# Output projection accumulated in PSUM, convolution evicted by ScalarE, mixes in six pieces, weight splits with priority

## Chip, cores and metric

One Trainium2 core runs the whole block. The metric is the time of one execution on the device in microseconds; every run was taken on the chip. The engines are TensorE (PE, and PEld for its weight loads), VectorE (DVE), ScalarE (ACT), GpSimd (POOL) and the DMA queue of SyncE (SP). Each engine takes its instructions in the order of its own queue and waits on semaphores at the head of it.

## The reference

A layer over 1024 tokens of width 1024 (float32), cut to what is computed:

```python
h = rmsnorm(x, g_pre_mix)
u, xc, bc, cc, q, k, v, f_logit, gate_logits = split(h @ w_in)
y_a = s5_mixer(u, ...)                       # complex diagonal scan, GELU, GLU
y_b = bc * conv3_causal(cc * xc, conv_w)     # short gated convolution, width 512
y_c = forgetting_attention(q, k, v, f_logit) # 8 heads of 64, causal
gates = sigmoid(gate_logits + b_gate)        # three times 1024 columns
merged = gates[0] * (y_a @ wa) + gates[1] * (y_b @ wb) + gates[2] * (y_c @ wc)
mix = merged @ w_out
x = x + rmsnorm(mix, g_post_mix)
h = rmsnorm(x, g_pre_mlp)
return x + rmsnorm(square(relu(h @ w_ff1)) @ w_ff2, g_post_mlp)
```

## The kernel before

Products are made from split operands: ScalarE writes the upper part of a weight or activation (a copy to fp32r), VectorE subtracts it from the source to get the lower part (`split`, line 72; `wsplit` for weights, line 204), and TensorE adds three products, upper with upper, upper with lower and lower with upper. A product is 128x128 by 128x512. A weight tile can be used in full only when its lower part is there.

The order is written out by a small planner. Phases are Python generators; `spawn(gen, delay)` enters one into an event queue, `poll` (line 102) runs what is due by a clock that counts modelled TensorE time alone, and a number that a generator yields is the delay of its next piece. `settle` runs all that is left. What is written in this order is then ordered again for each engine by the framework's scheduler, which goes by its own model of readiness and by priority (by default, earlier written is higher). Under `manual_schedule` the named engines keep the written order among the instructions of that block.

The stages, in order of time:

- To about 60 us: the 8 tiles of x (128 tokens each) are squared and summed, the reciprocal root comes from `rsqrt1` (line 79: eight small operations), `x_norm` (338) makes a diagonal matrix for each tile, and `x_tr` (361) multiplies by it, which scales and transposes at once. `x_split` writes hT, the transposed input, as upper and lower halves.
- To about 375 us: the input projections for u, then conv x, c, b and the gates through `proj_stream`, in two PSUM banks (tag `pj`), while the four quarters of S5 run beside them. `conv_cons` (799) empties the banks of the convolution: x by ScalarE; c by a VectorE multiplication with x; b by a VectorE multiplication with the convolved `ac`. GpSimd makes tables and some of the S5 operands.
- 375 to 430 us: the value projection (`v_group`, 869), under a manual order for VectorE and ScalarE, with 16 steps of gate projections ahead of the second weight split. A step is three products.
- To about 815 us: attention by 64 units, with the q, k and gate projections as filler for TensorE, and w_ff2's sums on GpSimd.
- To about 1005 us: the merge. `merge_item` (1217) takes two blocks of 128 columns of one branch: 24 products, then VectorE multiplies by the gate (loaded as `gl`), GpSimd adds to `ma`, and after the third branch the sum is split into mT. Between the merges of the first and the second half of the tokens stands the output projection of the first half, four `rows_item`s (1257) with four token tiles each: the first half of the contraction is copied by ScalarE to `acc`, the second is added to it by VectorE. There are 8 PSUM banks (`mps`, 1157).
- `mix` (1282) is spawned for each token tile after its projection: ScalarE's sum of squares and a root on GpSimd, scaling by g_post_mix, adding x, a second root, scaling to `hr`, and transposes. For the second half (`th` = 1) it also makes the operands T1 to T4 and B22 of the MLP.
- From 1005 us: the second half's output projection (two `rows_item`s and `wo_last`, 1357), then the MLP in a Strassen-like scheme over pairs of column blocks (`Pair`, 1429): first P1 and P2 of eight pairs (`prep_a`, `run_a`), which need only the first half, then the other products. From 1386 us the second matrix and the final norm.

`Item.split` (1191) splits a stage's weights; `run_items` (1196) splits item i+1 before item i runs and loads two ahead. Upper and lower weight tiles have three buffers each, raw weights two (tag `raw`).

Of the kernel before, what the change touches and what calls it, by code (L numbers as in the profile page):

```python
# [20 lines left out]
P = 128  # L21
# [17 lines left out]
def hybrid_layer(ctx, tc, a, out, dbg=None):  # L39
# [298 lines left out]
    def x_norm(t0, n):  # L338

        sl = slice(t0, t0 + n)  # L340
        rsqrt1(xrs[:, sl], xsq[:, sl], xtm[:, sl])
        for t in range(t0, t0 + n):
            dgs[t] = xp.tile([P, P], F, name=f"dg{t}", tag="dg", bufs=8)
            if t == 3:
                act.activation(dgs[t], ident, AF.Copy, scale=xrs[:, t:t + 1])
            else:
                ts(dgs[t], ident, xrs[:, t:t + 1], MUL)
# [24 lines left out]
    with tc.manual_schedule(engines={mybir.EngineType.DVE, mybir.EngineType.Activation}):  # L372
        for t in range(4):
            x_square(t)
            if t == 3:
# [14 lines left out]
        x_norm(4, 4)  # L390
# [408 lines left out]
    def conv_cons(which, j):  # L799
        def f(th, ps):  # L800
            sl = slice(th * HALF, (th + 1) * HALF)
            if which == "x":
                if th == 0:
                    cvt["xs"] = cv.tile([P, L], F, name=f"xs{j}", tag="xs")
                act.activation(cvt["xs"][:, sl], ps, AF.Copy)
            elif which == "c":
                if th == 0:
                    cvt["vp"] = cv.tile([P, L + 2], F, name=f"vp{j}", tag="vp")
                    pool.memset(cvt["vp"][:, 0:2], 0.0)
                vp = cvt["vp"]  # L810
                tt(vp[:, 2 + th * HALF:2 + (th + 1) * HALF], ps, cvt["xs"][:, sl], MUL)
                if th == 1:
                    ac = cvt["ac"] = cv.tile([P, L], F, name=f"ac{j}", tag="ac")
# [367 lines left out]
    class Item:  # L1181
# [33 lines left out]
    macc = {}  # L1215

    def merge_item(th, dp, b):
        def run(w):
# [15 lines left out]
            for d in range(2):  # L1234
# [16 lines left out]
                if b == 2:  # L1251
                    split(mT[0, th, dt_ // 4][:, dt_ % 4, :], mT[1, th, dt_ // 4][:, dt_ % 4, :], macc[d], scale=0.5)
# [4 lines left out]
    def rows_item(name, src_k, k0, e, toks, lhs, accumulate, after=None):  # L1257

        def run(w):
            for t in toks:  # L1260
                ps = mps(f"{name}p{t}")
                for k in range(4):
                    wh, wl = w[k // 2]
                    xh, xl = lhs(t, k)
                    mm(ps, xh, wh[:, k % 2, :], k == 0, False, 0.214)
                    mm(ps, xh, wl[:, k % 2, :], False, False, 0.214)
                    mm(ps, xl, wh[:, k % 2, :], False, k == 3, 0.214)
                dst = accs[t][:, e * HALF:(e + 1) * HALF]
                if accumulate:
                    tt(dst, ps, dst, ADD)  # L1270
                else:
                    act.activation(dst, ps, AF.Copy)
# [9 lines left out]
    def mix(t):  # L1282
# [10 lines left out]
        sp.dma_start(xr_, a["x"][t * P:(t + 1) * P, :])  # L1293
        hr = hrow[0](f"hr{t}")
        rs = rms_scale(acc, hr, f"n1_{t}")
        stt(acc, acc, rs, mixg[0], MUL, MUL)
        tt(acc, acc, xr_, ADD, dve if th else pool)
        yield MY1 if th else 8.0
        rs2 = rms_scale(acc, hr, f"n2_{t}")
        act.dma_start(x1_s[t], acc)  # L1300
        stt(hr, acc, rs2, mixg[1], MUL, MUL)
        c0 = (t % 4) * P
        cs = slice(c0, c0 + P)
        yield MY2 if th else 12.0
# [15 lines left out]
        else:  # L1320
# [22 lines left out]
    MY1, MY2 = 9.0, 12.0  # L1343
# [483 lines left out]
```

## Time and profile before

| | us |
|---|---|
| median of 3 runs | 1694.05 (1692.35 to 1694.09) |
| profiled execution | 1695.55 |
| its span, first to last instruction | 1693.8 |

The profile is of one execution. Its views are: the page with each engine's busy time; the waits, which put an engine's idle time down to what released it; windows, which give busy time and TensorE's granted clock (1.00 is 2.4 GHz, 0.50 is 1.2 GHz) of a stretch; the timeline of one engine, with the idle time ahead of an instruction and its releaser in brackets; groups by line; and the chain of work that ended last. Matmuls overlap, so the time of one is read from a long run of them.

### The profile page before, as it was taken

The numbers are of one execution on the slowest core, as the hardware profiler recorded it, in microseconds if no ns is written. First come the engines' busy times: TensorE is split into PE (matmuls) and PEld (weight loads), VectorE is DVE, ScalarE is ACT, GpSimd is POOL, SyncE is SP. The second block draws the span as 40 slices with busy tenths as digits, with TensorE's granted clock in tenths as the row PEclk, the third lists the DMA queues.
The fourth block names the chain that finished last, engine by engine and source line by source line (L and its number), as shares of the span: only waits on it lengthen the run. The fifth ranks groups of instructions, "written<-read, shape, count | busy, mean of one in ns | idle before, by whom it ended". The sixth has DMA issues, their size and how long they took to land.

```text
span 1693.8 us, 21052 instructions
## 1 busy us (share of the span) xinstructions
PE 1622.6 (96%) x7815; PEld 1334.8 (79%) x7815; DVE 1032.2 (61%) x1548; ACT 693.6 (41%) x1042; POOL 501.9 (30%) x603
## 2 busy tenths in 40 slices
PE   7999999999999999999999988799999999999997
PEld 6778778879878787877787777678778878888886
DVE  4768655333265463667583664778988764545665
ACT  5312122231354454556352333554354554444442
POOL 1085644100331403120153543244443300101143
PEclk9999999999999999999999989899999999999999
DMA  5412323330654616441782562456554599755521
GB/s 162 122 42 77 83 68 103 108 99 7 216 174 142 213 47 218 117 168 58 255 262 97 193 205 91 138 163 189 183 181 143 166 344 373 254 199 195 178 100 50
DMA packets 186034, 261.73 MB, mean 155 GB/s; under 512 B 24752, under 2 KB 108764, under 8 KB 183884
## 3 DMA queue, kind: packets, MB, share of 16 engines
q1 hardware_dynamic: 170380, 228.93, 41.8%
q10 hardware_dynamic: 15552, 31.46, 4.9%
q8 instruction: 61, 1.00, 0.2%
q14 instruction: 41, 0.34, 0.1%
HBM read 183.54 MB, written 75.63 MB: 153 GB/s over the span
## 4 chain that ended last, share of the span: by engine, by line
PE 64%; DVE 9%; POOL 5%; DMA 5%; issue 4%; ACT 3%; SPq 1%; DVEq 0%; ACTq 0%; POOLq 0%
PE p_g L122 13%; PE P L122 11%; PE pb L122 3%; PE p_q L122 3%; PE pv L122 3%; PE P4f L122 3%; PE P7f L122 3%; PE P3f L122 3%; PE P6f L122 3%; PE P5f L122 3%; PE P2f L122 3%; PE P1f L122 2%; PE ps L122 2%; PE av L122 2%; PE pt L126 2%
## 5 line engine op out<-in xcount | busy, mean ns | idle before, releaser
L65 DVE TENSOR_TENSOR st<-x,st 128x1024 fp32r<-128x1024 f32 x70 | 86.7, 1250 | 77.4 <-ACT st L73 74.4
L122 PE MATMUL p_g<-hT,w_g_1H 128*128 128x512 f32 x384 | 126.4, 407 | 5.1 <-ACT g L831 3.5
L122 PE MATMUL p_g<-hT,w_g_0H 128*128 128x512 f32 x384 | 126.9, 406 | 2.8 <-DVE ac L65 2.8
L73 ACT ACTIVATE st<-x 128x1024 fp32r<-128x1024 f32 x70 | 73.6, 1059 | 98.5 <-PE P6f L122 16.6
L65 POOL TENSOR_TENSOR w2s<-w2s 128x512 f32<-128x512 f32 x32 | 44.0, 1375 | 232.1 <-DMA w2s<-in_w_ff 232.1
L65 POOL TENSOR_TENSOR s<-w1r 128x512 f32<-128x512 f32 x32 | 52.4, 1659 | 167.4 <-DMA w1r<-in_w_ff 156.4
L122 PE MATMUL pb<-yH,wb_0L 128*128 128x512 f32 x192 | 77.5, 403 | 11.8 <-DVE wb_0L L65 11.7
L65 DVE TENSOR_TENSOR sl<-x,sh 128x1024 fp32r<-128x1024 f32 x42 | 56.6, 1352 | 47.4 <-ACT sh L73 47.4
L122 PEld LDWEIGHTS p_g<-hT,w_g_1H 128*128 128x128 f32 x384 | 69.3, 192 | 17.5 <-ACT g L831 4.0
L122 PEld LDWEIGHTS p_g<-hT,w_g_0H 128*128 128x128 f32 x384 | 70.0, 191 | 14.8 <-DVE ac L65 3.2
L122 PE MATMUL pb<-yH,wb_0H 128*128 128x512 f32 x192 | 77.0, 401 | 2.1 <-DVE macc L68 2.1
L65 POOL TENSOR_TENSOR fa<-fa,gfin 128x512 f32<-128x512 f32 x16 | 25.5, 1606 | 178.0 <-ACT fjk L1654 178.0
L122 PE MATMUL p_g<-hT,w_g_1L 128*128 128x512 f32 x192 | 76.6, 399 | 0.0
L122 PE MATMUL pb<-yL,wb_0H 128*128 128x512 f32 x192 | 76.6, 399 | 0.0
L122 PE MATMUL p_g<-hT,w_g_0L 128*128 128x512 f32 x192 | 76.5, 398 | 0.0
L65 DVE TENSOR_TENSOR PT<-pt,PT 128x512 fp32r<-128x512 f32 (+2 forms) x96 | 53.0, 552 | 26.7 <-ACT PT L73 26.1
L73 ACT ACTIVATE PT<-pt 128x512 fp32r<-128x512 f32 (+2 forms) x96 | 47.0, 490 | 47.9 <-PE pt L126 43.5
L73 ACT ACTIVATE sh<-x 128x1024 fp32r<-128x1024 f32 x42 | 44.2, 1058 | 51.4 <-PE P3f L122 9.9
L1023 ACT ACTIVATE P<-ps,mx 128x128 f32<-128x128 f32 (+3 forms) x64 | 47.4, 740 | 32.0 <-DVE mx L1020 31.9
L65 POOL TENSOR_TENSOR macc<-macc,gl 128x512 f32<-128x512 f32 x16 | 27.8, 1748 | 101.6 <-DVE gl L68 101.6
L1020 DVE TENSOR_REDUCE mx<-ps 128x1 f32<-128x128 f32 (+3 forms) x64 | 48.1, 752 | 13.2 <-PE ps L122 13.1
L122 PEld LDWEIGHTS pb<-yH,wb_0L 128*128 128x128 f32 x192 | 37.0, 193 | 21.7 <-DVE wb_0L L65 13.9
(831 smaller groups left out, 4631.6 us busy)
## 6 DMA issues: line engine op xcount, KB each, us to landing
w2s<-in_w_ff SPq DMA_DIRECT2D x16, 1024.0 KB, 5.0
w1r<-in_w_ff SPq DMA_DIRECT2D x16, 1024.0 KB, 8.6
as<-sa SPq DMA_DIRECT2D x16, 1024.0 KB, 6.8
x<-as SPq DMA_DIRECT2D x32, 512.0 KB, 10.8
x<-t_P SPq DMA_DIRECT2D x32, 512.0 KB, 5.3
r_g<-in_w_in SPq DMA_DIRECT2D x12, 1024.0 KB, 5.9
gt_s<-g ACTq DMA_DIRECT2D x48, 256.0 KB, 2.0
t_P<-w2s SPq DMA_DIRECT2D x48, 256.0 KB, 2.6
```

Source lines behind the costliest of these rows:

```text
L65: (eng or dve).tensor_tensor(o, x, y, op=op)
L73: act.activation(hi, src, AF.Copy, scale=scale)
L122: pe.matmul(o, l, r, start=start, stop=stop)
L126: pe.transpose(o, i, idn)
L1020: dve.tensor_reduce(mx, sv, axis=mybir.AxisListType.XY, op=MAX, negate=True)
L1023: act.activation(Pm[:, 0:kend].rearrange("p (c n) -> p c n", c=nch), sv, AF.Exp, bias=mx, accum_out=sm)
```

## The change

- Input: the roots are made one at a time for the first four tiles, that of tile 1 by GpSimd; the first weight split has its subtraction on VectorE instead of GpSimd. Tiles 4 to 7 are scaled in place (two by VectorE, two by ScalarE) and transposed with the identity.
- Convolution: ScalarE copies c and b out of PSUM; VectorE multiplies whole rows of 1024 in SBUF. The buffers are three, two and two in place of one each.
- Value projection: 12 gate steps ahead of the first weight split and 20 ahead of the second, where 0 and 16 were.
- `Item.split` and `prep_a` split under `high_priority`.
- The split of a merged block is an event of its own, 2 us after the sum was written.
- The output projection keeps its sum in PSUM over both halves of the contraction and is copied to `acc` once, by ScalarE.
- `mix` yields five times instead of two; T4 takes one VectorE operation less; the rows `hr` of tiles 6 and 7 no longer lie in a raw weight buffer but share two buffers with the others.
- P1 and P2 of the first eight pairs run two pairs at a time (`ff1_early`) with the same products, and `settle` follows them.

```diff
+    def x_rs(t0, n, eng=None):
         sl = slice(t0, t0 + n)
-        rsqrt1(xrs[:, sl], xsq[:, sl], xtm[:, sl])
+        rsqrt1(xrs[:, sl], xsq[:, sl], xtm[:, sl], eng)
...
-        mm(o, xt[t][:, kt * P:(kt + 1) * P], dgs[t], True, True, 0.22)
+        if t < 4:
+            mm(o, xt[t][:, kt * P:(kt + 1) * P], dgs[t], True, True, 0.22)
+        else:
+            transp(o, xt[t][:, kt * P:(kt + 1) * P], ident)
...
             x_square(t)
-            if t == 3:
-                ut_tiles[0].split(pool)
-            x_norm(t, 1)
+            x_rs(t, 1, pool if t == 1 else None)
             if t == 0:
+                x_diag(0)
                 dve.tensor_copy(gcol, pgc[:, 0:KT])
+            elif t == 2:
+                x_diag(1)
+                x_diag(2)
+        ut_tiles[0].split()
+        x_diag(3)
...
-        x_norm(4, 4)
+        x_rs(4, 4)
+        for t in range(4, NT):
+            if t % 2:
+                ts(xt[t], xt[t], xrs[:, t:t + 1], MUL)
+            else:
+                act.activation(xt[t], xt[t], AF.Copy, scale=xrs[:, t:t + 1])
...
-                tt(vp[:, 2 + th * HALF:2 + (th + 1) * HALF], ps, cvt["xs"][:, sl], MUL)
+                act.activation(vp[:, 2 + th * HALF:2 + (th + 1) * HALF], ps, AF.Copy)
                 if th == 1:
+                    tt(vp[:, 2:], vp[:, 2:], cvt["xs"], MUL)
...
-                ac = cvt["ac"]
-                tt(ac[:, sl], ps, ac[:, sl], MUL)
+                if th == 0:
+                    cvt["bs"] = cv.tile([P, L], F, name=f"bs{j}", tag="xs", bufs=3)
+                act.activation(cvt["bs"][:, sl], ps, AF.Copy)
                 if th == 1:
+                    ac = cvt["ac"]
+                    tt(ac, ac, cvt["bs"], MUL)
...
+        for _ in range(12):
+            next(ps_)
         split(wv[1][1], wv[1][2], wv[1][0])
-        for _ in range(16):
+        for _ in range(20):
             next(ps_)
...
-                self.w = [wsplit(self.raw[ix], shp, f"{self.name}_{i}") for i, (ix, shp) in enumerate(self.cuts)]
+                with tc.high_priority():
+                    self.w = [wsplit(self.raw[ix], shp, f"{self.name}_{i}") for i, (ix, shp) in enumerate(self.cuts)]
...
-                    split(mT[0, th, dt_ // 4][:, dt_ % 4, :], mT[1, th, dt_ // 4][:, dt_ % 4, :], macc[d], scale=0.5)
+                    spawn(merged(mT[0, th, dt_ // 4][:, dt_ % 4, :], mT[1, th, dt_ // 4][:, dt_ % 4, :], macc[d]), 2.0)
...
-                ps = mps(f"{name}p{t}")
+                if k0 == 0:
+                    wps[t, e] = mps(f"{name}p{t}")
+                ps = wps[t, e]
...
-                dst = accs[t][:, e * HALF:(e + 1) * HALF]
-                if accumulate:
-                    tt(dst, ps, dst, ADD)
-                else:
-                    act.activation(dst, ps, AF.Copy)
+                if k0:
+                    act.activation(accs[t][:, e * HALF:(e + 1) * HALF], ps, AF.Copy)
...
         sp.dma_start(xr_, a["x"][t * P:(t + 1) * P, :])
+        yield 1.5
         hr = hrow[0](f"hr{t}")
         rs = rms_scale(acc, hr, f"n1_{t}")
+        yield 5.0
         stt(acc, acc, rs, mixg[0], MUL, MUL)
         tt(acc, acc, xr_, ADD, dve if th else pool)
-        yield MY1 if th else 8.0
+        yield 2.5 if th else 5.0
         rs2 = rms_scale(acc, hr, f"n2_{t}")
         act.dma_start(x1_s[t], acc)
+        yield 5.0
         stt(hr, acc, rs2, mixg[1], MUL, MUL)
         c0 = (t % 4) * P
         cs = slice(c0, c0 + P)
-        yield MY2 if th else 12.0
+        yield 5.0
...
-            tt(tm[:, 1], b12, tk["D"][:, :, cs], ADD)
             tt(tm[:, 0], b22, tb[:, 1], SUB)
             tt(tb[:, 0], b22, tb[:, 0], SUB)
-            stt(tm[:, 1], b22, -1.0, tm[:, 1], MUL, ADD)
+            tt(tm[:, 1], tk["D"][:, :, cs], tb[:, 0], SUB)
...
-                    dst = accs[t][:, e * HALF:(e + 1) * HALF]
-                    tt(dst, ps, dst, ADD)
+                    act.activation(accs[t][:, e * HALF:(e + 1) * HALF], ps, AF.Copy)
...
-    hrow[0] = hr_tile
-    stages = ff1_stages()
+    hrow[0] = lambda name: r2.tile([P, D], F, name=name, tag="hr", bufs=2)
+    pairs = [Pair(i) for i in range(NF)]
+    stages = ff1_stages(pairs)
...
+    for i in range(0, KC, 2):
+        nxt = [p.prep_a for p in pairs[i + 2:i + 4]] if i + 2 < KC else [s_[0] for s_ in stages[:AH]]
+        for _ in ff1_early(pairs[i:i + 2], nxt):
+            poll()
+    settle()
```

## Rows read from the trace of the kernel before

**Rows 1.** The page: the span, then section 1, busy time of each engine.

```profile
span 1693.8 us, 21052 instructions
PE 1622.6 (96%) x7815; PEld 1334.8 (79%) x7815; DVE 1032.2 (61%) x1548; ACT 693.6 (41%) x1042; POOL 501.9 (30%) x603
```

**Rows 2.** Whom TensorE waited for: us in total, times, longest us.

```profile
PE P L122 <- DVE wa1L L65: 11.9, 1, 11.9
PE pb L122 <- DVE wb_0L L65: 11.7, 4, 7.2
PE p_cb L122 <- DVE vp L65: 3.7, 2, 2.6
PE p_g L122 <- ACT g L831: 3.5, 1, 3.5
PE p_g L122 <- DVE ac L65: 2.8, 1, 2.8
PE p_cx L122 <- DVE ac L65: 2.7, 1, 2.7
```

**Rows 3.** Windows: length; busy PE, PEld, DVE, ACT, POOL; granted clock; DMA.

```profile
111.50:115.00 3.50, 3.50 (x11) 2.68 (x10) 3.50 (x3) 0.00 (x0) 3.34 (x4) 0.52 0.05 11
206.60:210.00 3.40, 3.38 (x9) 2.73 (x10) 3.40 (x10) 0.20 (x1) 0.00 (x0) 0.60 0.39 160
251.00:254.50 3.50, 3.50 (x11) 2.69 (x11) 0.94 (x1) 0.00 (x0) 3.03 (x10) 0.59 0.80 251
373.00:377.00 4.00, 3.83 (x12) 3.03 (x13) 3.15 (x2) 1.86 (x3) 0.00 (x0) 0.69 0.57 160
926.50:930.50 4.00, 3.80 (x10) 2.98 (x11) 1.76 (x3) 0.00 (x0) 2.09 (x7) 0.62 0.41 131
979.50:985.30 5.80, 5.68 (x13) 4.47 (x14) 3.18 (x5) 1.12 (x3) 2.29 (x8) 0.50 0.91 314
1066.20:1071.50 5.30, 5.25 (x17) 4.18 (x18) 3.02 (x3) 2.25 (x5) 4.41 (x10) 0.56 0.77 201
84.00:88.00 4.00, 4.00 (x11) 3.14 (x10) 3.79 (x15) 0.00 (x0) 0.00 (x0) 0.53 0.06 18
```

**Rows 4.** Timeline of TensorE: start us, us; diagonal products, then transposes.

```profile
39.37 5.56 PE L122 MATMUL ptx<-dg,x 128*128 128x128 f32 x48
...
1070.68 1.11 PE L126 MATMUL pth<-ident,hr 128*128 128x128 f32 x8
```

**Rows 5.** Timeline of ScalarE before the second half is transposed; idle before in brackets.

```profile
38.20 0.69 ACT L369 ACTIVATE hT<-ptx,gcol 128x512 fp32r<-128x512 f32 x1 [4.87 <-PE ptx L122]
```

**Rows 6.** Timeline of VectorE in the convolution.

```profile
108.09 1.59 DVE L65 TENSOR_TENSOR CA<-CA,Cx 128x1152 f32<-128x1152 f32 x1 [6.26 <-POOL Cx L65]
```

**Rows 7.** Groups of ScalarE, 60 to 370 us: busy us, mean ns, idle before.

```profile
L805 ACT ACTIVATE xs<-p_cx 128x512 f32<-128x512 f32 x8 | 4.7, 590 | 19.9 <-PE p_cx L122 19.9
```

**Rows 8.** Timeline of ScalarE ahead of the value projection.

```profile
370.57 1.96 ACT L73 ACTIVATE wvH<-r_wv 128x2112 fp32r<-128x2112 f32 x1 [9.42 <-DMA ya_s<-so]
```

**Rows 9.** Timeline of VectorE in the merge of the second half.

```profile
973.42 2.27 DVE L68 SCALAR_TENSOR_TENSOR acc<-acc,n_3r,gpost 128x1024 f32<-128x1024 f32 x1 [2.73 <-POOL n_3r L62]
...
976.21 3.35 DVE L65 TENSOR_TENSOR wb_0L<-r_wb,wb_0H 128x1024 fp32r<-128x1024 f32 x1
```

**Rows 10.** Timeline of VectorE as the MLP begins.

```profile
1063.78 1.28 DVE L68 SCALAR_TENSOR_TENSOR acc<-acc,n_7r,gpost 128x1024 f32<-128x1024 f32 x1 [2.88 <-POOL n_7r L62]
1064.98 1.22 DVE L65 TENSOR_TENSOR wa1L<-w1h,wa1H 128x1024 fp32r<-128x1024 f32 x1
```

**Rows 11.** Timeline of GpSimd in a chain of small operations.

```profile
1056.08 1.43 POOL L62 TENSOR_SCALAR n_5t<-n_5r,n_5q 128x1 f32<-128x1 f32 x1
...
1058.00 0.34 POOL L62 TENSOR_SCALAR n_5t<-n_5r,n_5q 128x1 f32<-128x1 f32 x1
```

**Rows 12.** Whom ScalarE waited for, 900 to 1130 us.

```profile
ACT wb_0H L73 <- DMA r_wb<-in_w_branch: 10.9, 2, 5.9
```

**Rows 13.** Chain that ended last: start us, us, what.

```profile
1641.82 43.53 PE P4f L122 x192
```

More of the change, by code (lines that the diff above doesn't have):

```diff
@@ L336, in x_square, with x_diag @@
         act.activation(jk, xt[t], AF.Square, accum_out=xsq[:, t:t + 1])
-    def x_norm(t0, n):
+    def x_rs(t0, n, eng=None):
         sl = slice(t0, t0 + n)
-        rsqrt1(xrs[:, sl], xsq[:, sl], xtm[:, sl])
-        for t in range(t0, t0 + n):
-            dgs[t] = xp.tile([P, P], F, name=f"dg{t}", tag="dg", bufs=8)
-            if t == 3:
-                act.activation(dgs[t], ident, AF.Copy, scale=xrs[:, t:t + 1])
-            else:
-                ts(dgs[t], ident, xrs[:, t:t + 1], MUL)
+        rsqrt1(xrs[:, sl], xsq[:, sl], xtm[:, sl], eng)
+    def x_diag(t):
+        dgs[t] = xp.tile([P, P], F, name=f"dg{t}", tag="dg", bufs=4)
+        if t == 3:
+            act.activation(dgs[t], ident, AF.Copy, scale=xrs[:, t:t + 1])
+        else:
+            ts(dgs[t], ident, xrs[:, t:t + 1], MUL)
     pxs = {}
@@ L1215, in hybrid_layer, with merged @@
     macc = {}
+    def merged(hi, lo, m):
+        split(hi, lo, m, scale=0.5)
+        yield 0.0
     def merge_item(th, dp, b):
@@ L1255, in merge_item, with rows_item @@
                     [((FULL,), [4, 256])], run)
-    def rows_item(name, src_k, k0, e, toks, lhs, accumulate, after=None):
+    wps = {}
+    def rows_item(name, src_k, k0, e, toks, lhs, after=None):
         def run(w):
             for t in toks:
-                ps = mps(f"{name}p{t}")
+                if k0 == 0:
+                    wps[t, e] = mps(f"{name}p{t}")
+                ps = wps[t, e]
                 for k in range(4):
@@ L1342, in hybrid_layer @@
     EXTK = ("B22", "T1", "T2")
-    MY1, MY2 = 9.0, 12.0
+    MS = 0.0
     WP = (5, 0)
@@ L1353, in wo_item @@
         last = kc == 1 and e == 1
-        return rows_item(f"wo{th}{kc}{e}", wo_k, 4 * kc, e, range(4 * th, 4 * th + 4), lhs, kc == 1,
+        return rows_item(f"wo{th}{kc}{e}", wo_k, 4 * kc, e, range(4 * th, 4 * th + 4), lhs,
                          (lambda t: spawn(mix(t), 10.0 * (t % 4))) if last else None)
@@ L1366, in run @@
                 for e in range(2):
-                    ps = mps(f"wl{t}{e}")
+                    ps = wps[t, e]
                     for k in range(4):
@@ L1370, in run @@
                         xh, xl = lhs(t, k)
-                        mm(ps, xh, wh, k == 0, False, 0.214)
+                        mm(ps, xh, wh, False, False, 0.214)
                         mm(ps, xh, wl, False, False, 0.214)
                         mm(ps, xl, wh, False, k == 3, 0.214)
-                    dst = accs[t][:, e * HALF:(e + 1) * HALF]
-                    tt(dst, ps, dst, ADD)
+                    act.activation(accs[t][:, e * HALF:(e + 1) * HALF], ps, AF.Copy)
                     if e:
-                        spawn(mix(t))
+                        spawn(mix(t), MS * (t % 4))
                     if (t, e) == WP:
-                        stages[0][0]()
+                        pairs[0].prep_a()
                     yield
@@ L1438, in prep_a @@
                 raw = w1_load(i)[:, :, 0:P]
-            self.wa = wsplit(raw, [KT, P], f"wa{i}")
+            with tc.high_priority():
+                self.wa = wsplit(raw, [KT, P], f"wa{i}")
         def prep_b1(self):
@@ L1478, in run_a, with run_p1, run_p2 @@
             yield
+        def run_p1(self):
+            i = self.i
+            if i % 2 == 0:
+                s1t[i // 2] = lt.tile([P, 2, HALF], F, name=f"s1_{i}", tag=f"acc{(i // 2) % 4}")
+            self.s1 = s1t[i // 2][:, i % 2]
+            self.p1 = prod(f"P1_{i}", self.wa, 0, h2[0, 0], h2[1, 0])
+            act.activation(self.s1, self.p1, AF.Copy)
+        def run_p2(self):
+            i = self.i
+            p2 = prod(f"P2_{i}", self.wa, 4, h2[0, 1], h2[1, 1])
+            o = lt.tile([P, HALF], F, name=f"o11_{i}", tag="row", bufs=3)
+            tt(o, p2, self.s1, ADD)
+            put_a(i, "P1", o)
+            self.a11 = None
         def run_b1(self):
@@ L1522, in run_b3, with ff1_early, ff1_stages @@
             yield
-    def ff1_stages():
-        ps_ = [Pair(i) for i in range(NF)]
+    def ff1_early(p, nxt):
+        p[0].run_p1()
+        nxt[0]()
+        yield
+        p[0].run_p2()
+        yield
+        p[1].run_p1()
+        nxt[1]()
+        yield
+        p[1].run_p2()
+        yield
+    def ff1_stages(ps_):
         A = lambda p: [(p.prep_a, p.run_a)]
@@ L1528, in ff1_stages @@
         st = []
-        for p in ps_[:KC]:
-            st += A(p)
         for p in ps_[:KC]:
@@ L1740, in hybrid_layer @@
     r2 = r2_es.enter_context(pool_("r2"))
-    hlate = []
-    def hr_tile(name):
-        t = int(name[2:])
-        if t < 6:
-            return r2.tile([P, D], F, name=name, tag="hr", bufs=2)
-        if not hlate:
-            hlate.append(ws.tile([P, 2, D], F, name="hr67", tag="raw", bufs=2))
-        return hlate[0][:, t - 6, :]
-    hrow[0] = hr_tile
-    stages = ff1_stages()
+    hrow[0] = lambda name: r2.tile([P, D], F, name=name, tag="hr", bufs=2)
+    pairs = [Pair(i) for i in range(NF)]
+    stages = ff1_stages(pairs)
     run_items(wo1[:1], wo1[1:])
@@ L1760, in hybrid_layer @@
     AH = 2
-    for s_ in range(1, AH):
-        stages[s_][0]()
+    pairs[1].prep_a()
+    for i in range(0, KC, 2):
[3 more added lines that the diff above has]
+    settle()
     for n, (_, run) in enumerate(stages):
@@ L1767, in hybrid_layer @@
             stages[n + AH][0]()
-        if n == KC:
-            settle()
         to_end = len(stages) - n
```

13 lines of the change are left out of this document (6 added, 7 removed).

## The prediction

> **What bounds the kernel now.** I read the page first: TensorE is busy for 1622.6 of 1693.8 us, VectorE for 61% and ScalarE for 41% [rows 1]. So a microsecond is won only where TensorE stands still, where it does fewer products, or where it runs at its lower clock; relieving VectorE is worth nothing by itself. The second view is therefore whom TensorE waited for [rows 2], and the reader is to see two things there. The stalls are few and long, and nearly all end with a VectorE instruction whose own cost is small. Third come the windows right behind the long stalls [rows 3]: after a stall the granted clock is near 0.5 (1.2 instead of 2.4 GHz) for three to six microseconds with TensorE busy, so a stall costs its length and then (1 - clock) times such a window. Last I looked into the queue of the engine named, to see what stood in front of the late instruction.
>
> Three of the six places are one pattern: an in-order queue whose head waits. In the convolution VectorE idles 6.26 us for GpSimd's table products, and the multiplication that empties a PSUM bank stands behind it [rows 6]. In the merge VectorE idles 2.73 us for the reciprocal root of mix 3, is then slowed to 2.27 us in the scaling, and only then does the weight split that TensorE needs [rows 9]. As the MLP begins it is the same: 2.88 us of waiting for mix 7's root, then the split of the second weight [rows 10], for which TensorE had stood 11.9 us.
>
> **The sum, part by part.** It is made against the profiled execution, 1695.55 us (1.75 us of it outside the span); the median of the runs is 1.5 us lower.
>
> *A, input transposes.* Tiles 4 to 7 are scaled in place and transposed plainly; before, each was multiplied by a diagonal. A diagonal product shows as two records: 48 records (24 products) take 5.56 us, 0.116 each, and 8 transposes, one record each, 1.11 us, 0.139 with their drain [rows 4]. 32 products lose 32 records: 32 x 0.116 = 3.7 us, and I take 3.5. Added are four scalings of 1024 columns, two on each engine. On ScalarE that is about 2 x 2 x 0.59 = 2.4 us by its copies of 512 columns [rows 7]; it idles 4.87 us right there [rows 5], so the price is nothing, and 2.4 us if the cover fails. The clock is the other bound. At 84 to 88 us TensorE ran at 0.53 [rows 3], and what it did just before was 40 small transposes; the same behind these would cost 0.47 x 4 = 1.9 us. Bounds: a gain of 3.7 down to a loss of 0.6; **3.5**. At the very start one root of four goes to GpSimd and the first split from GpSimd to VectorE. That trades a shorter chain for a slower one; bounds 0.6 us gained to 1 us lost, by a GpSimd operation of 0.34 against 1.43 us [rows 11]; value 0.
>
> *B, convolution.* ScalarE now empties both the c and the b banks. The x banks are emptied so already, 8 copies of 0.59 us, and no wait of TensorE names them [rows 2, 7]. The multiplications by VectorE stay, but no bank hangs on them. At stake are 3.7 + 2.8 + 2.7 = 9.2 us of waits [rows 2], and the slow windows behind three of them, 0.48 x 3.5 + 0.40 x 3.4 + 0.41 x 3.5 = 4.5 us [rows 3]: 13.7. The S5 chain on VectorE and GpSimd runs through the same time and gets no shorter, so TensorE may meet it later; bounds 7 (half) to 13.7, **10**, nearer the upper end because no wait of TensorE here names an S5 result [rows 2]. The 16 new ScalarE copies, 9.4 us in all, lie beside products: the group already idles 19.9 us for TensorE [rows 7].
>
> *C, value projection.* ScalarE stood 9.42 us at the head of its queue with the first value split, whose buffer waited for a write to DRAM [rows 8]; two gate banks were full behind it and TensorE stopped for 3.5 us, then ran at 0.69 for 4 us [rows 2, 3]. Twelve gate steps now stand ahead of that split, so their evictions are not behind it: 3.5 + 1.2 = 4.7, **4.5**. But 32 steps in place of 16 are taken from the filler of the attention. 16 steps are 48 products; at 43.53 / 192 = 0.227 us [rows 13] that is 10.9 us which attention must fill otherwise. Early merge products can follow into its end. Bounds 0 to 10.9 lost, **2 lost**, since no wait on an attention operand stands among the six [rows 2].
>
> *D, output projection, mixes and merge, first half.* Keeping the sum in PSUM removes 16 ScalarE copies and turns 16 VectorE additions into ScalarE copies; the products are the same in number. For itself it is worth nothing. Eight banks are then held, all that there are, until the second half of the contraction. The mixes go in six pieces: the scaling is issued only 5 us after its root was started, and the split of a merged block 2 us after its sum, so VectorE meets them when they are ready. Item splits have priority. The loads of a mix still go through SP ahead of the gates and weights, as before. At stake: 11.7 us in four waits [rows 2], and 0.38 x 4 + 0.50 x 5.8 = 4.4 us of slow clock [rows 3], 16.1. I take three quarters, **12**. The rest stays because a split that meets a GpSimd addition in flight takes 3.35 us [rows 9] against 1.22 without [rows 10], and four mixes bring four such additions.
>
> *E, mixes of the second half beside the first MLP products.* The evictions no longer read what VectorE wrote, the second weight's split has priority, and the spare buffer of the last two mixes no longer takes a weight buffer. At stake: 11.9 + 0.44 x 5.3 = 14.2 us [rows 2, 3]. Against it: the row buffers are two instead of four, so mix 6 starts only when mix 4 has been transposed, and VectorE has more work in these 45 us than anywhere. Bounds 5 to 14.2, **10.5**.
>
> Sum: -3.5 - 10 - 4.5 + 2 - 12 - 10.5 = -38.5. From 1695.55 that gives 1657.0, and 1655.5 on the scale of the median: **1655 us**. With every upper end it is 1694 - 3.7 - 13.7 - 4.7 - 16.1 - 14.2 = 1642; with the lower ends (A +0.6, B -7, C +6.4, D -8, E -5) it is 1681.
>
> **The rivals.** *GpSimd takes the place of VectorE.* All sixteen roots of the mixes are chains on GpSimd. One of their operations takes 1.43 us instead of 0.34 when it meets VectorE [rows 11]. If VectorE no longer idles, it meets more of them: one more hit for each chain is 16 x 1.09 = 17 us, of which D and E give back most, say 13: 1668 us. For it: VectorE already waits for these roots at both places [rows 9, 10]. Against it: the pieces leave 5 us between root and use.
> The Trainium skill (SBUF — State Buffer, section "Who interferes with whom") says that VectorE with two SBUF inputs and a GpSimd instruction that reads SBUF exclude each other for the whole instruction, whoever is first. The rows of 3.35 and 1.43 us agree with that; by that rule priority only chooses who waits, which is this rival and its 1668.
>
> *The change doesn't do what it says in the mixes*: the order that the scheduler makes is the old one in effect, because its model of GpSimd is faster than the chip. Then only A, B and C count: 1694 - 3.5 - 10 - 2.5 = 1678 us.
>
> *Slower: ScalarE's head waits for loads.* Priority puts a split at the head of ScalarE's queue, and evictions now stand behind it. Twice it stood there for a weight load, 10.9 us in all, the longest 5.9 us [rows 12]. A merge item feeds TensorE for 24 x 0.227 = 5.4 us [rows 13], so a wait of 5.9 with only the subtraction of 1.22 us behind it [rows 10] already starves it by 1.7 us. There are 38 item splits and 16 in the MLP, 54. D and E's 22.5 us are then not won, and A to C keep 16. From 16 / 54 = 0.3 us lost for each split on, the kernel is slower; at 0.6 us it is 1694 - 16 + 32 = 1710 us. Against it: loads are asked for two items ahead, and only two such waits stand in the trace.
>
> **How the numbers follow.** Forecast with its bounds 1645 to 1666: 0.50; better than that, 1642 and about it: 0.08; GpSimd, 1668: 0.18; old order, 1678: 0.13; a result near the start, within 0.2% (about what a measurement of this kernel can tell from no change): 0.04; slower, 1710: 0.07. The range 1641 to 1680 leaves out the last two and the edges of the others. Faster: 0.50 + 0.08 + 0.18 + 0.13 = 0.89.
>
> **What would show it.** A: 32 records fewer of the diagonal products and no slow window near 45 us. B: no wait on vp or ac. C: no wait on a gate eviction near 370 us; a gap in TensorE between 770 and 815 us would show the missing filler. D and E: no wait of more than 2 us on a weight's lower half, and a granted clock of 1.0 from 920 us on. I am wrong if VectorE's or ScalarE's queue has new heads waiting for GpSimd or a load, if TensorE waits at the eight banks as a projection begins, or if the S5 products become what it waits for.

## The result and the profile after

The changed kernel takes 1677.0 us (median; 1675.5 to 1678.6) against 1693.2 (1690.5 to 1694.1) of the kernel before, a ratio of 0.9907 (0.989 to 0.9924). That is 16 us less; 38.5 were forecast. Its profiled execution is 1678.55 us long.

The page of the changed kernel, the span and section 1, busy time of each engine; it answers to [rows 1].

```profile
span 1676.8 us, 20962 instructions
PE 1613.7 (96%) x7783; PEld 1331.5 (79%) x7783; DVE 1024.1 (61%) x1511; ACT 703.4 (42%) x1060; POOL 514.8 (31%) x610
```

TensorE has 32 records fewer, as forecast for the transposes, and is busy 8.9 us less. Whom it waited for, us in total, times, longest; it answers to [rows 2].

```profile
PE pth L126 <- DVE hr L68: 12.9, 2, 7.2
PE pb L122 <- DVE wb_0L L65: 10.3, 5, 4.5
PE pb L122 <- DVE macc L68: 4.8, 2, 4.6
PE pz L122 <- DVE gq L68: 3.6, 1, 3.6
```

The waits on vp and ac and the 3.5 us for the gate g are gone. The 11.9 us for wa1L are gone too, and 12.9 us for hr, the row that a mix hands to its transposes, stand in their place. The 11.7 us for wb_0L are still 10.3, though the longest of these waits is 4.5 in place of 7.2. Apart from the start, two waits are clearly new or longer: pz, an S5 product, and macc, for which the line before was:

```profile
PE pb L122 <- DVE macc L68: 2.1, 1, 2.1
```

Where the 17 us of span came from can be read by landmarks: the start of the first product of each kind, and the time from one to the next. The last stretch, from the first P1f product that reads an st slice to the end, is 305.3 us in every kernel of this study. The other rows scatter more, between profiles of kernels whose code is the same in that stretch: products of u begin between 16.4 and 19.1 us; A's stretch differs by 0.6 us, B's by 2.4 (159.2 to 161.6), C's by 3.5 (543.7 to 547.2), the two merge rows by about 2 each, and that of the first MLP layer by 0.7. Smaller differences mean nothing.

| stretch (us) | before | after | change |
|---|---|---|---|
| start to the first product of u | 17.3 | 19.0 | +1.6 |
| u to the convolution (A) | 64.8 | 60.2 | -4.6 |
| convolution to the first gate (B) | 168.1 | 159.4 | -8.7 |
| gate to the first merge product (C and attention) | 549.9 | 545.0 | -4.9 |
| merge of the first half (D) | 74.2 | 77.8 | +3.6 |
| projection and merge of the second half (D) | 130.4 | 126.7 | -3.7 |
| projection of the second half (D) | 43.5 | 44.5 | +1.0 |
| first MLP layer with the mixes (E) | 340.2 | 338.9 | -1.4 |
| second MLP layer | 305.3 | 305.3 | 0 |

(The changes are taken before rounding.) In this profile A, B and C came about as forecast or better. D (12 forecast) came to nothing and E (10.5 forecast) to 1.4 us.

### The profile page after: what moved, and what is told of

Read it like the earlier page. It is cut to its first block, busy times and chain, and to the rows that moved or that the text cites. A ratio compares the mean times of both kernels' runs of the same rounds, so it can differ in the third digit from the quotient of the medians.

```text
span 1676.8 us, 20962 instructions
## 1 busy us (share of the span) xinstructions
PE 1613.7 (96%) x7783; PEld 1331.5 (79%) x7783; DVE 1024.1 (61%) x1511; ACT 703.4 (42%) x1060; POOL 514.8 (31%) x610
## 4 chain that ended last, share of the span: by engine, by line
PE 43%; DVE 7%; issue 4%; POOL 3%; ACT 2%; DMA 2%; SPq 0%; DVEq 0%; ACTq 0%; POOLq 0%
PE P L122 13%; PE P4f L122 3%; PE P3f L122 3%; PE P6f L122 3%; PE P5f L122 3%; PE P2f L122 3%; PE P7f L122 3%; PE P1f L122 2%; PE p_g L122 2%; PE pb L122 1%; PE wo101p L122 1%; PE wo100p L122 1%; PE ps L122 1%; PE p_q L122 1%; PE av L122 1%
## 5 line engine op out<-in xcount | busy, mean ns | idle before, releaser
L122 PE MATMUL pb<-yH,wb_0L 128*128 128x512 f32 x192 | 77.1, 401 | 10.3 <-DVE wb_0L L65 10.3
L122 PEld LDWEIGHTS p_g<-hT,w_g_1H 128*128 128x128 f32 x384 | 69.6, 189 | 11.7 <-issue 0.2
L848 ACT ACTIVATE g<-p_g,bgcol 128x512 f32<-128x512 f32 x48 | 32.8, 683 | 53.4 <-PE p_g L122 53.2
```

Source lines behind the costliest of these rows:

```text
L122: pe.matmul(o, l, r, start=start, stop=stop)
L848: act.activation(g, ps, AF.Tanh, bias=bgcol[:, i:i + 1], scale=0.5)
```

## Experiments

All ratios are to the kernel before on the same chip, with 95% intervals; they are collected in one table, and what each run tells stands below.

| run | edit | us, median | ratio |
|---|---|---|---|
| e1_abc | before, with A, B, C alone | 1676.7 | 0.9912 (0.9891 to 0.9933) |
| e2_only_b | before, with B alone | 1682.2 | 0.9943 (0.9924 to 0.9962) |
| e3_only_c | before, with C alone | 1690.5 | 0.9997 (0.9982 to 1.0011) |
| e4_gates16 | after, 12 + 4 gate steps | 1685.3 | 0.9958 (0.9942 to 0.9974) |
| e5_no_prio | after, no priority | 1673.8 | 0.9888 (0.9871 to 0.9906) |
| e6_roots_dve | after, 16 roots on VectorE | 1677.6 | 0.9903 (0.9886 to 0.992) |
| e7_late_tr | after, later transposes | 1679.8 | 0.9924 (0.9908 to 0.9939) |
| e8_old_start | after, the old start | 1679.0 | 0.992 (0.9903 to 0.9937) |
| e9_roots4 | after, 8 roots on VectorE | 1674.7 | 0.9892 (0.9874 to 0.991) |
| e10_roots4_np | e9 without priority | 1663.9 | 0.9842 (0.982 to 0.9864) |
| e11_junk | after, squares' output elsewhere | 1674.3 | 0.9892 (0.9875 to 0.9909) |
| e12_junk_roots4_np | e10 and e11 together | 1659.2 | 0.9808 (0.9787 to 0.9828) |
| e13_prio_items | e12, priority for merge and projection | 1670.6 | 0.9867 (0.9846 to 0.9888) |
| e14_prio_wa | e12, priority for the MLP's weights | 1661.7 | 0.9812 (0.9794 to 0.9831) |
| e15_roots8 | e12, all 16 roots on VectorE | 1659.4 | 0.9805 (0.9788 to 0.9823) |
| e16_abc_roots4 | e1, 8 roots on VectorE | 1668.4 | 0.9862 (0.9843 to 0.9882) |

### The first three parts by themselves

e1 takes the diff's parts for input, convolution and value projection into the kernel before, e2 the convolution alone, e3 this alone:

```diff
+        for _ in range(12):
+            next(ps_)
         split(wv[1][1], wv[1][2], wv[1][0])
-        for _ in range(16):
+        for _ in range(20):
             next(ps_)
```

> The kernel before with the input transposes, the convolution and the value projection of the change (A, B, C) and nothing of D and E. Theory 1 (the landmarks of the two traces: A 3.0 us, B 5.8, C about 8, D and E together nothing): 16 to 18 us less than before, 1675 to 1678, the same as the changed kernel within 2 us. Rival (D and E do win 4 to 10 us, and something of C loses it again): 1681 or more. Old-order rival of the prediction: 1678, with no sign of a difference in the merge.

> The kernel before with the convolution's evictions on ScalarE alone. Theory (landmarks between first and last product of the convolution): 5 to 7 us less, 1686 to 1688, the waits on vp and ac gone and a new wait on the S5 product gq of 3 to 4 us. The prediction's term: 10 us less, 1683. Rival (the S5 chain takes all of it back): within 2 us of 1693.

> The kernel before with the value projection's order alone (12 gate steps ahead of the first value split, 20 ahead of the second). The prediction's term: 2.5 us less, 1690.5. Theory from the landmarks: about 8 us less, 1685, because the attention doesn't miss the filler. Rival (the missing filler shows at the end of the attention or in the first merge): 1691 to 1696.

e1 is as fast as the whole change: what D and E add together is nothing, within the interval. e2 gains 9.7 us, the prediction's 10, and more than the 5 to 7 that I had read between the first and the last convolution product; the wait on the S5 product that I expected in it is there (3.1 us for gq), so part of the 13.7 at stake did come back later, as the term allowed. e3 missed the 8 that I had read off two traces: 0.5 us by the ratio, between a gain of 3.0 and a loss of 1.9. The prediction's 2.5 lies inside; a clear gain of C by itself isn't shown. No run has A alone: e1 gains 15.2 us by the medians and e2 9.7, which leaves 5.5 for A and C together (3.5 and 2.5 forecast).

e4 takes back the sixteen extra gate steps:

```diff
-        for _ in range(20):
+        for _ in range(4):
             next(ps_)
```

> The changed kernel with 12 gate steps ahead of the first value split and 4 ahead of the second, 16 in all as before, so 16 steps more are left as filler for the attention. Theory (the longer stall at the start of the merge, 4.58 us on macc at 816 us with 3 us at half clock behind it, comes from the missing filler): 4 to 7 us less than the changed kernel, 1670 to 1673. Rival 1 (the stall comes from the order that priority made, whatever the filler): 1676 to 1678. Rival 2 (with 4 steps the second value split is waited for): 1680.

It is 8 us slower than the changed kernel, and the wait on macc is still 5.0: the missing filler isn't the cause of that stall. Its second rival, a wait for the second value split, is what came. Whom TensorE waited for in e4, 340 to 470 us:

```profile
PE pv L122 <- ACT wvH L73: 3.4, 1, 3.4
PE pv L122 <- DVE zf L65: 3.0, 1, 3.0
PE pv L122 <- DVE wvL L65: 1.6, 1, 1.6
```

These are 8.0 us, and the stretch from the first gate to the first merge product is 551.0 us in place of 545.0. The twenty steps are the cover under which the second value split is made. A loss of filler by the attention, as I had it, isn't seen: in the changed kernel this stretch, which contains the attention, is 4.9 us shorter than before, as much as C's stall of 4.7 was.

### The start

e8 puts the start back to what it was:

```diff
-            x_rs(t, 1, pool if t == 1 else None)
+            x_rs(t, 1)
...
-        ut_tiles[0].split()
+        ut_tiles[0].split(pool)
```

> The changed kernel with the start as before (root of tile 1 on VectorE, the first weight's subtraction on GpSimd). Theory (the diagonal of tile 1 comes 2.0 us later in the changed kernel, 12.78 against 10.80 us): the first product of u starts at 17.3 instead of 19.0 us and the whole is 1 to 2 us shorter, 1675 to 1676. Rival (the gain is given back at the next tile that has to be loaded): within 1 us of the changed kernel.

It is not faster. Its products of u begin at 17.6 us, those of e10, with the new start, at 16.4. So the 1.6 us that the changed kernel's profile shows there are no price of the change: 0.6 of them are the arrival of a tile of x (its square starts at 8.18 us after, 7.57 before), and the rest differs between executions of the same code.

### The roots of the mixes

In the changed kernel VectorE still stands where it stood. Timeline of VectorE in the merge of the second half, start us, us, idle before in brackets; it answers to [rows 9].

```profile
958.21 2.27 DVE L68 SCALAR_TENSOR_TENSOR acc<-acc,n_3r,gpost 128x1024 f32<-128x1024 f32 x1 [2.70 <-POOL n_3r L62]
960.40 1.21 DVE L65 TENSOR_TENSOR wb_0L<-r_wb,wb_0H 128x1024 fp32r<-128x1024 f32 x1
...
968.12 1.28 DVE L68 SCALAR_TENSOR_TENSOR hr<-acc,n_3r,gmlp 128x1024 f32<-128x1024 f32 x1 [3.73 <-POOL n_3r L62]
```

The head of the queue is the same instruction, its wait is 2.70 in place of 2.73 us, and the split stands behind it again, six pieces or two. So e6 moves all sixteen roots to VectorE (first pair of lines) and e9 the eight of the first half, n1 and n2 alike (second pair):

```diff
-        rsqrt1(rs, sq, tm, pool)
+        rsqrt1(rs, sq, tm)
...
-        rs = rms_scale(acc, hr, f"n1_{t}")
+        rs = rms_scale(acc, hr, f"n1_{t}", pool if th else None)
```

> The changed kernel with the sixteen roots of the mixes on VectorE instead of GpSimd; TensorE's queue is the same, instruction for instruction. Theory (GpSimd's root is the step that holds VectorE, and so the transposes: 3.0 to 5.0 us for a chain there, 1.9 us on VectorE by the first root of the kernel): two mixes in series give 4 roots x 2 us = 8 us and the slow clock behind, 8 to 14 us less than the changed kernel, 1663 to 1669, the stalls before the transposes shorter by half. Rival 1 (VectorE gets 16 x 1.9 = 31 us more work at its busiest place): 1677 to 1685. Rival 2 (what holds the transposes is their place in TensorE's queue and the two row buffers, not the roots): within 3 us of 1677.

> The changed kernel with the eight roots of the first half's mixes (those that run beside the merge of the second half) on VectorE, those of the second half on GpSimd as they are; TensorE's queue is the same. Theory (with all sixteen on VectorE the waits on wb_0L, 10.3 us, were gone and the MLP's start lost as much): the merge keeps its gain and the MLP's start stays at 12.9 us, 7 to 12 us less than the changed kernel, 1665 to 1670. Rival 1 (TensorE arrives earlier at the MLP and stands there instead, since the mixes of the second half are no earlier): 1674 to 1678. Rival 2 (GpSimd's additions of the merge go slower beside it): 1675 or more.

TensorE's queue is the same in all three, so only waits differ. Whom TensorE waited for in e6:

```profile
PE pth L126 <- DVE hr L68: 17.2, 4, 10.2
PE pth L126 <- DVE n_7q L62: 7.2, 1, 7.2
PE pb L122 <- DVE macc L68: 4.9, 2, 4.7
```

No wait on wb_0L is left of 10.3 us, which is what the theory says; the stretch of the projection and second merge falls from 126.7 to 122.9 us. But the total is the same as after: 3.4 us more are lost in the first MLP layer (342.2). e9 keeps 122.7 in the merge and gains 2.3 us in the total, a third of the least that I expected and less than the intervals resolve. In the merge, where wb_0L is gone, TensorE now waits 7.9 us in two places for hr, the row of a mix of the first half.

### Priority

e5 takes the priority away in both places, e10 does that to e9:

```diff
-                with tc.high_priority():
-                    self.w = [wsplit(self.raw[ix], shp, f"{self.name}_{i}") for i, (ix, shp) in enumerate(self.cuts)]
+                self.w = [wsplit(self.raw[ix], shp, f"{self.name}_{i}") for i, (ix, shp) in enumerate(self.cuts)]
...
-            with tc.high_priority():
-                self.wa = wsplit(raw, [KT, P], f"wa{i}")
+            self.wa = wsplit(raw, [KT, P], f"wa{i}")
```

> The changed kernel without priority for the weight splits. Theory (D and E win nothing because what TensorE waits for hangs on GpSimd's roots and on the row buffers, and priority doesn't touch those): within 3 us of the changed kernel, 1674 to 1680, the two transposes of 5.7 and 7.2 us still waiting. Rival 1 (priority holds off worse): over 1682. Rival 2 (priority made the stall at 816 us, 4.58 us and 3 us of half clock): 1670 to 1672.

> The same without priority for the weight splits. Theory (priority is worth nothing once VectorE's head no longer waits, and it costs the stall of 4.6 us on macc at 816 us): 2 to 5 us less than with it, 1661 to 1667. Rival (priority is what keeps wb_0L off): 3 us more or worse, with waits on wb_0L of 4 us or more.

By itself priority is worth nothing or a little less: e5 is 3.2 us below the changed kernel, and the intervals overlap. It moves waits about. Whom TensorE waited for in e5:

```profile
PE pb L122 <- DVE wb_0L L65: 11.4, 4, 7.2
PE pb L122 <- DVE macc L68: 2.2, 1, 2.2
```

Behind mix 3's scaling (at 957.38 us in e5) the split comes second without priority and takes 3.36 us; with it the split comes first and takes 1.21, so the longest wait on wb_0L is 4.5 in place of 7.2. What that gains, macc loses: 4.8 in place of 2.2.

With the roots on VectorE priority costs 8.5 us by the ratios and 10.8 by the medians (e9 against e10). And without priority the roots alone are worth 7.8 us by the ratios (e10 against e5), with TensorE's queue the same in both. The start of the merge shows how priority costs. VectorE's timeline of the changed kernel there:

```profile
805.08 1.28 DVE L68 SCALAR_TENSOR_TENSOR macc<-gl,pb 128x512 f32<-128x512 f32 x2
810.26 2.29 DVE L65 TENSOR_TENSOR yL<-yr,yH 128x2048 fp32r<-128x2048 f32 x1 [3.90 <-ACT yH L73]
812.48 1.22 DVE L65 TENSOR_TENSOR wb_0L<-r_wb,wb_0H 128x1024 fp32r<-128x1024 f32 x1
813.61 0.68 DVE L68 SCALAR_TENSOR_TENSOR macc<-gl,pb 128x512 f32<-128x512 f32 x1
814.21 1.22 DVE L65 TENSOR_TENSOR wb_0L<-r_wb,wb_0H 128x1024 fp32r<-128x1024 f32 x1
815.34 0.68 DVE L68 SCALAR_TENSOR_TENSOR macc<-gl,pb 128x512 f32<-128x512 f32 x1
```

The same place in e5, which reaches the merge 1.6 us later:

```profile
811.05 1.23 DVE L65 TENSOR_TENSOR wb_0L<-r_wb,wb_0H 128x1024 fp32r<-128x1024 f32 x1 [3.01 <-ACT wb_0H L73]
813.34 1.43 DVE L68 SCALAR_TENSOR_TENSOR macc<-gl,pb 128x512 f32<-128x512 f32 x2 [1.07 <-DMA gl<-gt_s]
814.69 2.29 DVE L65 TENSOR_TENSOR yL<-yr,yH 128x2048 fp32r<-128x2048 f32 x1
```

The two multiplications into macc empty the only two banks that the merge has there (tag `pj`). Without priority they stand ahead of yL; with it they stand behind yL, which waits 3.90 us for a load of the attention's output (ScalarE's yH, 5.53 us for yr from yc_s), and behind two weight splits. TensorE waits 4.6 us there (2.2 in e5) and then runs at its lower clock. Priority also changes TensorE's own order: 44 of its 7783 products, between 787 and 797 us, where the last of the attention and the first of the merge meet. No run separates the two. Windows of the changed kernel, the first behind this stall, the other two behind those of the next section: length, busy PE, PEld, DVE, ACT, POOL, granted clock, DMA.

```profile
816.00:819.50 3.50, 3.33 (x8) 2.67 (x9) 0.02 (x1) 0.00 (x0) 0.00 (x0) 0.53 0.80 268
1050.00:1055.00 5.00, 4.70 (x16) 4.08 (x17) 4.88 (x8) 2.69 (x6) 1.27 (x3) 0.52 0.00 0
1066.00:1072.00 6.00, 5.84 (x18) 5.00 (x19) 6.00 (x9) 4.08 (x7) 5.31 (x9) 0.51 0.35 136
```

In landmarks e10 against e9: first merge 73.2 against 78.6 us, projection and second merge 119.1 against 122.7. With the roots moved and no priority, e10 gains what D was to win: from the first merge product to the MLP 235.9 us, 248.1 before. Whom TensorE waited for in e10:

```profile
PE pth L126 <- DVE hr L68: 17.1, 3, 8.3
PE pb L122 <- DVE macc L68: 2.1, 1, 2.1
PE pb L122 <- DVE wb_0L L65: 1.6, 1, 1.6
```

### The row buffers and TensorE's head

As the MLP begins, TensorE waits in the changed kernel twice for a row. Its timeline:

```profile
1050.30 1.97 PE L126 MATMUL pth<-ident,hr 128*128 128x128 f32 x8 [5.72 <-DVE hr L68]
1066.16 1.94 PE L126 MATMUL pth<-ident,hr 128*128 128x128 f32 x8 [7.20 <-DVE hr L68]
```

VectorE's timeline ahead of the first of them, with the row of mix 5 in the second line; it answers to [rows 10]:

```profile
1043.82 1.29 DVE L68 SCALAR_TENSOR_TENSOR acc<-acc,n_6r,gpost 128x1024 f32<-128x1024 f32 x1 [3.48 <-POOL n_6r L62]
...
1048.96 1.29 DVE L68 SCALAR_TENSOR_TENSOR hr<-acc,n_5r,gmlp 128x1024 f32<-128x1024 f32 x1 [2.59 <-POOL n_5r L62]
```

And GpSimd's, with the root that VectorE waits for:

```profile
1043.87 1.29 POOL L62 TENSOR_SCALAR n_5q<-n_5q 128x1 f32<-128x1 f32 x1
1045.25 1.17 POOL L62 TENSOR_SCALAR n_5r<-n_5q 128x1 int32<-128x1 int32 x1
...
1048.63 0.29 POOL L62 TENSOR_SCALAR n_5r<-n_5t,n_5r 128x1 f32<-128x1 f32 x1
```

Mix 5's second root takes 5.0 us on GpSimd; but it starts only at 1043.87, though mix 5's sum was there at 1031.8. ScalarE's timeline tells why (the lines with L1195 are squares, hr is their unused output; the first is mix 6's, the second mix 5's, the third mix 7's):

```profile
1034.64 0.59 ACT L1401 ACTIVATE acc<-wo101p 128x512 f32<-128x512 f32 x1
1035.75 0.60 ACT L1513 ACTIVATE s<-P 128x512 f32<-128x512 f32 x1 [0.52 <-PE P L122]
1038.03 1.06 ACT L73 ACTIVATE wa3H<-w1h 128x1024 fp32r<-128x1024 f32 x1 [1.69 <-PE P L122]
1039.06 0.64 ACT L1442 ACTIVATE o<-o 128x512 f32<-128x512 f32 x1
1039.60 1.04 ACT L1195 ACTIVATE hr<-acc 128x1024 f32<-128x1024 f32 x1
1041.16 1.05 ACT L1195 ACTIVATE hr<-acc 128x1024 f32<-128x1024 f32 x1
...
1052.31 1.06 ACT L1195 ACTIVATE hr<-acc 128x1024 f32<-128x1024 f32 x1 [4.36 <-PE pth L126]
```

Mix 6's square has its operand at 1028.2, but it writes into the row buffer that mix 4's transposes free at 1039.1, so it stands in the queue behind the first evictions of the MLP; mix 5's stands behind it and starts 9.4 us after its operand was ready. (From 1042.3 us on mix 5's root stands behind mix 6's on GpSimd.) The second stall has the same head, and there the wait itself shows: mix 7's square holds ScalarE 4.36 us for the transposes of mix 5, and mix 6's second square, behind it, starts 9.5 us after its operand was ready. e7 writes the transposes later (first pair of lines); e11 gives the squares another place for their unused output:

```diff
-        yield 5.0
+        yield 12.0 if th else 5.0
         pts = []
...
-        hr = hrow[0](f"hr{t}")
-        rs = rms_scale(acc, hr, f"n1_{t}")
+        jk = r2.tile([P, 2, 4, P], F, name=f"jk{t}", tag="tm", bufs=2).rearrange("p a k f -> p (a k f)") if th else hrow[0](f"hr{t}")
+        rs = rms_scale(acc, jk, f"n1_{t}")
...
-        rs2 = rms_scale(acc, hr, f"n2_{t}")
+        rs2 = rms_scale(acc, jk, f"n2_{t}")
...
+        hr = hrow[0](f"hr{t}") if th else jk
         stt(hr, acc, rs2, mixg[1], MUL, MUL)
```

> The changed kernel with the transposes of the second half's mixes written 12 in place of 5 us behind their scaling, so that they stand behind more products in TensorE's queue. Theory (the stalls of 5.7 and 7.2 us as the MLP begins are TensorE's own head waiting for a row that isn't there yet): these 13 us and 3 us of slow clock go, 1661 to 1667. Rival (the chain through two row buffers and GpSimd's roots is what ends late; with later transposes the buffers come free later and the same time is lost at the end of the P1 and P2 products, at about 1085 us): 1674 to 1682.

> The changed kernel with the unused output of the squares of the second half's mixes written into a buffer of another tag, so that a mix's first square no longer waits for a row buffer (until the mix two before it has been transposed) and the second square of mix 5 no longer stands behind the first of mix 6 in ScalarE's queue. Theory (the two row buffers are why E won nothing): the two waits before the transposes, 12.9 us and 3 us of slow clock, shrink to 4 or less, 1662 to 1668. Rival 1 (GpSimd's roots alone are late enough): waits of 9 us or more, 1673 to 1678. Rival 2 (VectorE has too much to do between 1015 and 1080 us in any order): a new wait on a weight's lower half, 1673 or more.

e7 came as its rival said: 8.9 us of waiting in place of 12.9, nothing gained in the total, and 340.3 us of first MLP layer against 338.9; moving the head of the queue only moves the time. In e11 the waits for hr are gone from this stretch but for 0.5 us. Whom TensorE waited for in e11, 1030 to 1100 us:

```profile
PE pth L126 <- ACT s L1514: 2.3, 1, 2.3
PE P L122 <- DVE o L65: 2.1, 1, 2.1
PE P L122 <- DVE wa1L L65: 1.4, 1, 1.4
...
PE pth L126 <- DVE hr L68: 0.5, 1, 0.5
```

The stretch falls from 338.9 to 333.9 us. The total shows 2.7 us of it, not the 9 to 15 that I expected. It lies in the range of both rivals, but the sign of neither is there: 0.5 us for hr, 1.4 for a weight's lower half. Small waits came in, on evictions and splits.

e12 joins e10 and e11, e15 also moves the last eight roots to VectorE, e13 and e14 give priority back to one kind of split each.

> Both: the roots of the first half on VectorE, the squares' unused output out of the row buffers, no priority. If the merge's loss and the MLP's are separate things, the gains add: 1650 to 1658. If they hang together (one end sets when the other begins): no more than the better of the two alone, 1662 to 1668.

> The combined kernel (roots of the first half on VectorE, squares' unused output out of the row buffers; 1659 us without any priority) with priority for the weight splits of merge and projection alone. Theory (it is these that put a waiting load ahead of what empties the merge's banks): 5 to 10 us more, 1664 to 1669, with the wait on macc of about 5 us back at the start of the merge. Rival (they are harmless, the MLP's splits cost): 1657 to 1661.

> The combined kernel with priority for the first weights of the MLP alone. Theory (6.6 us of waiting for wa1L stand in the combined kernel without priority, and nothing else hangs on it): 4 to 8 us less, 1651 to 1655. Rival (priority there puts a split that waits for its load ahead of the mixes): 1659 to 1664.

> The combined kernel without priority, with the roots of the second half on VectorE as well; TensorE's queue is the same. If GpSimd's roots are what the mixes of the second half wait for: 3 to 8 us less, 1651 to 1656. If VectorE is full there (four mixes of about 14 us and eight weight splits of 1.2 us in some 60 us): 2 to 6 us more, 1661 to 1665.

The gains add, roughly: e12 is at 1659.2 us, 32.4 below the kernel before on that chip (1691.6) and just outside the 1650 to 1658 that I expected. e13 shows which priority costs: that of merge and projection, 10 us by the ratios, with 5.2 us on macc. e14 is as e12: the wait for wa1L shrinks from 6.6 to 1.5 us and the MLP's stretch from 334.6 to 331.8, but the total doesn't show it: none of the 4 to 8 us of my theory came, and the time lies in the rival's range, whose reason is not shown. e15 met neither of its forecasts: the time is the same with all roots on VectorE, so VectorE is not full there, though one transposition then waits 9.8 us for a root.

### Was D's own part worth anything?

e16 is e1 with the eight roots of the first half on VectorE: mixes in two pieces, the sum of the projection by VectorE, no priority.

> The kernel before with A, B and C (1676.7 us) and the roots of the first half on VectorE; the mixes in two pieces, the projection's sum by VectorE, no priority. Theory (what D was to win is the engine of the roots; pieces and sum in PSUM are worth nothing by themselves): 10 to 13 us less, 1664 to 1667, waits on wb_0L of 2 us or less. Rival (the two-piece mix issues its scaling at once, so VectorE waits there for its own chain and the pieces are needed): 1670 to 1676.

8.5 us less than e1 by the ratios, with TensorE's queue the same in both: the engine of the roots alone brings most of D. It is less than the 10 to 13 that I expected, and not all of the wait on wb_0L went; it was to be 2 us or less:

```profile
PE pb L122 <- DVE wb_0L L65: 5.5, 2, 5.1
```

e10, which has the pieces and the sum in PSUM besides, is 3.4 us lower, but the intervals overlap; in landmarks 2.7 lie between the first merge product and the MLP (235.9 against 238.6), where profiles of the same code differ by 2, and 1.5 in the first MLP layer. So a small part of the pieces is likely and not shown.

## Why the prediction was right and wrong

**What bounds the kernel**: right. Beside A's fewer products, the gains that the runs show come with waits of TensorE, and the slow clock behind them, that went.

**A, B, C**: right in the sum, 15.2 us in e1 for 16. A was 4.6 us for 3.5: its stretch is 59.7 to 60.3 us in every kernel that has it and 64.0 to 64.9 without it, so its bound of 3.7 was at best just enough. B was 8.7 by landmarks and 9.7 alone, for 10. C's stall went (no wait on g), and its stretch is 4.9 us shorter, but alone it shows 0.5 with 3.0 as its best end. Its filler term looked at the wrong thing: no loss of filler is seen in the attention, and e4 shows that without the extra steps ahead of it the second split is waited for, at 8 us.

**D: the step that failed is "VectorE meets them when they are ready".** The pieces set when a scaling is written down, not what stands ahead of a split in VectorE's queue: the head at 958 us is that of [rows 9] and its wait 2.70 us. The prediction's own reading of [rows 9] named the root on GpSimd as the thing waited for, and the change leaves it there. With the roots on VectorE and no priority, this part gives 12.2 us (248.1 to 235.9), by another mechanism than the prediction's; that it is the 12 of the sum is luck. The second failed step is that priority was costed at nothing in D: it costs about 9 us in the landmarks of e9 against e10, 5.4 of them at the first merge.

**E: the step that failed is the price of "the row buffers are two instead of four".** It stood in the text, but inside a lower bound of 5. It held mix 6's square, behind it mix 5's, and so the transposes: the 11.9 us before the second weight became 12.9 before the transposes. e11 takes 5.0 us out of that stretch, which makes 6.3 against the kernel before (340.2 to 333.9), and e14, with priority for wa alone, makes 8.4. What keeps the rest of the 10.5 stays open; waits of up to 2.3 us stand in its place, and the totals show less than the stretch does.

**The rivals.** "The old order in effect" forecast 1678 and named what happened in the second merge; it had a chance of 0.13. e1 at 1676.7 says the same: A, B and C are all of the change's gain. Its reason was only half right, for priority did change the order, and lost at macc what it won on wb_0L. "GpSimd takes the place of VectorE" had the right engine and the wrong account: no further hits (12 of the 128 operations of the roots take over 0.9 us, before and after), but the old wait for the root in the merge, which nothing had removed. The Trainium skill's rule (SBUF — State Buffer, "Who interferes with whom"), that a VectorE instruction with two SBUF inputs and a GpSimd instruction that reads SBUF exclude each other, agrees with the 1.29 us of a GpSimd operation on one column beside a VectorE instruction of 1.29 us at 1043.8. What the runs add is that in the merge the engine of the roots decides; beside the MLP it made no difference (e15). "ScalarE's head waits for loads" came true at one place (5.53 us for yr from yc_s, 4.58 us of TensorE's time against 2.25 in e5), far from the 54 places by which it would have made the kernel slower.

**The three quarters and the bounds.** I took three quarters of what was at stake in D and E, with bounds of 8 and 5 below. Nothing in the rows supported a lower bound above zero: for each stall the text had a head of the queue, and for none did it show that the change takes that head away.

## What to carry to other kernels

When a stall is traced to an in-order queue, name the instruction at its head and what that waits for, and count a gain only if the change moves that thing; issuing it in smaller pieces, or ranking what stands behind it, left it at the head here. Priority for a prefetch puts it in front of the instruction that empties a bank: look at what it passes. An output that nobody reads still needs a buffer, and a buffer that is shared with a real result makes the next tile wait for this one's consumer.

## What was not expected of the hardware

The same chain of eight operations on one column takes 2.0 us on VectorE where nothing is queued between (954.01 to 956.04 us in e10), 3.0 us on GpSimd when it is alone (1026.23 to 1029.21 after), and 5.0 us beside VectorE (1043.87 to 1048.92). The second MLP layer took 305.3 us in all the profiled executions, while eighteen executions of the kernel before ranged from 1685.9 to 1697.0 us: the spread probably lies in what comes ahead, though only one of the eighteen was profiled.
